# A hybrid SSD layer on one core: the gate and norm of the scans' output taken chunk by chunk inside the scan

## The chip, the cores and the metric

The kernel runs on one core of one Trainium2 chip. The metric is the device time of one execution in microseconds; the time before is the median of three runs. Engines are named as in the profile: PE (matmuls), PEld (weight loads into PE), DVE, ACT, POOL, and SP, whose queue issues most DMAs.

## The reference

One layer is run for 256 context tokens (the "prompt", p) and 1024 latent tokens (the "sample", s) with shared weights. All is float32. The part that the change touches is the second half of the mixer:

```python
xs, bm, cm = silu(conv(xbc))          # 512 channels of X, 2 groups x 128 of B and of C
dt_f, dt_b = softplus(dt + bias)      # 8 heads each, forward and backward
y = ssd_scan(x, dt_f, ...) + reversed(ssd_scan(reversed x, dt_b, ...)) + x * d_skip
y = rmsnorm(y * silu(z), g_ssd_norm)  # over the 512 channels
out = concat([out_a, y]) @ w_out      # out_a = gb * conv(gc * hc)
```

hc, gb, gc, z, xbc and dt are columns of one projection h @ w_in. The scans go in chunks of 128 tokens. A gated ConvFFN follows.

## The kernel before

Channels lie on the 128 partitions and tokens along the free dimension. Every large matmul is made of three float32r matmuls on split operands: hi is the rounded copy (an ACT Copy), lo the remainder (a subtraction on DVE or POOL), and a product is hi x hi + hi x lo + lo x hi (`mm3`, L153 to L164). A weight tile is loaded by SP into "raw" (`wload`, L144) and split by ACT (L149) and by POOL or DVE (L75 under `tt`). L75 and L78 are the helpers `tt` and `stt`, so nearly all DVE work has one of these two lines and is told apart by tile names.

One projection is 24 tiles of w_in; `proj_halves` (L360) issues it in two halves of four k each, so that other work can be put between. For the prompt all projections run in one stage (L697 to L713): eight of xbc, four of z (`zproj`), twelve for the four outputs `outa` of the short convolution. `dtstage` (L448) turns dt into decays: a chain of ACT (Exp, Ln) and DVE operations with its own table load at L211. `dttok` (L500) turns the result token-major on PE and builds a diagonal on DVE (L515) for one more matmul (L518).

For the sample, xbc is projected first. The eight halves of z and the 24 halves of `outa` form a generator, `fillers` (L747), a list of 32 pieces of PE work that are drawn one by one between the steps of the scan: one piece for each pair of chunks in pass 1 (the backward states, L773), then in pass 2 (`ssd_pass2`, L583) two pieces for the first two steps of the prompt and one for every other step. Pass 2 has two steps i per chunk, one per group. A step draws its piece, runs `output` (L639, matmuls at L652 into the PSUM tile "yp", then X = X * d_skip + yp on DVE), asks for csb two or three steps on, and prepares the masked decays wm and csb of the step after next (`prep`, L622). What is left of the pieces runs after the scan (L779).

z goes to DRAM: `zproj_halves` copies it out of PSUM on ACT (L405) and stores it with a DMA on ACT's queue (L406) as zd[j, :, tokens], four tiles j of 128 channels. After the scan `gate` (L790) runs for the prompt and then for the sample, at high priority, while the leftover pieces still run on PE: per j it loads z (L795), takes Silu (L796), multiplies into X, squares on ACT (L799, L802) and sums on DVE; a matmul with a tile of ones sums over partitions (`rstd`, L215, matmul at L221, Ln at L224, Exp at L226, table load at L211). Then X = X * g * r on DVE and the split into hi (ACT, L813) and lo (DVE, L814) into the tiles "ya" and "yb" that the out-projection reads.

The out-projection `wout` (L856) uses a new PSUM pool, opened at L826 after the old one is closed. Its x tiles and the conv outputs (tiles "oa", "ob") are loaded by SP at L832 to L842, behind the stores of the conv outputs at L438 and L439 in program order. The order on each engine is made by the framework's scheduler from the order of the program, priorities, and the edges that `after` (L205) adds. A queue or engine works in order.

Of the kernel before, what the change touches and what calls it, by code (L numbers as in the profile page):

```python
# [13 lines left out]
P = 128  # L14
# [4 lines left out]
L = 128  # L19
# [34 lines left out]
def body(nc, tc, A):  # L54
# [38 lines left out]
    def smv(n):  # L93
        a, b = SMO[n]
        return sm[:, a:b]
# [176 lines left out]

    def ada_block(k):
        wa = [T(xy, [P, 4, 2 * P], "xs", 4) for _ in range(2)]
# [76 lines left out]
    zd = T(dr, [4, P, TT], "zd", 1)  # L351
# [47 lines left out]
    def zproj_halves(s, j, lo_eng):  # L399
        g = proj_halves(s, 12 + j, lo_eng)  # L400
        next(g)
        yield
        pp = next(g)
        z = T(cv, [P, s.T], "xl", 2)
        act(z, pp, AF.Copy)  # L405
        nc.scalar.dma_start(zd[j, :, s.t0:s.t0 + s.T], z)  # L406
        yield
# [175 lines left out]
    def ssd_pass2(s, fill):  # L583
# [83 lines left out]
        for i in range(2 * s.nc):  # L667
            behind = fill(s, i)
            if i % 2 == 1 and i + 1 < 2 * s.nc:
                u.step(behind)  # L670
            output(*us[i], behind)
            load(i + 3)
            if i + 2 < 2 * s.nc:
                if i % 2 == 0:
                    u = front(i // 2 + 1)
                us.append((u, i % 2))
                prep(*us[-1])
        if s.name == "p":
            dma(A["o_stf"], sf[0])
# [12 lines left out]
    SS.X = [T(xy, [P, TS], "xs", 4) for _ in range(4)]  # L692
# [11 lines left out]
    silu = act(bcall, bcall, AF.Silu)  # L704
    for j in range(4):
        zproj(SP, j, PG if j % 2 else PV)
        if j == 0:
            dts = dtstage(SP, d4_p, silu)
    for j in range(4):
        for _ in outa(SP, j, PG):  # L710
            pass
        if j == 0:
            dttok(SP, *dts)  # L713
    dts = dtstage(SS, d4_s, silu)
# [40 lines left out]
    def fill(s, i):  # L755

        for _ in range(2 if s.name == "p" and i < 2 else 1):
            next(filler)
        return mid_mm[0]
# [13 lines left out]
    for i in range(0, len(scan), 2):  # L773
        cps = pairs(scan[i:i + 2])
        next(filler)
        steps(cps, (mid_mm[0], last_mm[-1]))
    ssd_pass2(SP, fill)
    ssd_pass2(SS, fill)
# [8 lines left out]
    g_gt, gt_ = open_pool("gt")  # L787
    mya = [[T(ya, [P, TA], "ya", 8, F32R) for _ in range(2)] for _ in range(4)]
    myb = [[T(yb, [P, OB], "yb", 8, F32R) for _ in range(2)] for _ in range(4)]
    def gate(s, behind):  # L790
        n = s.T
        acc = T(gt_, [P, n], "gq", 3)
        for j in range(4):
            z = T(gt_, [P, n], "gz", 2)
            dma(z, zd[j, :, s.t0:s.t0 + n])  # L795
            act(z, z, AF.Silu)  # L796
            tt(s.X[j], s.X[j], z, ALU.mult)
            if j == 0:
                act(acc, s.X[j], AF.Square)  # L799
            else:  # L800
                q = T(gt_, [P, n], "gq", 3)
                sq = act(q, s.X[j], AF.Square)  # L802
                tt(acc, acc, q, ALU.add)
        r = T(gt_, [P, n], "gq", 3)
        rstd(r, acc, n, pst, 512, sq, behind)
        for j in range(4):
            y = s.X[j]
            stt(y, y, smv("gsd")[:, j:j + 1], r, ALU.mult, ALU.mult)
            parts = [(0, n, mya, s.t0)] if s.name == "p" else \
                [(0, TA - TP, mya, TP), (TA - TP, TS, myb, 0)]  # L810
            for a, b, dst, o in parts:
                hi = dst[j][0][:, o:o + b - a]
                act(hi, y[:, a:b], AF.Copy)  # L813
                tt(dst[j][1][:, o:o + b - a], y[:, a:b], hi.bitcast(F32), ALU.subtract)  # L814
    with tc.high_priority():
        gate(SP, last_mm[-5])
        gate(SS, last_mm[-3])
    close_pool(g_xy)

    close_pool(g_gt)  # L820
# [394 lines left out]
```

## Time and profile before

| | us |
|---|---|
| median of 3 runs | 1587.39 |
| lowest, highest run | 1586.29, 1590.08 |
| profiled execution | 1587.93 |
| its span, first to last instruction | 1586.1 |
| PE busy / DVE busy / ACT busy / POOL busy | 1530.3 / 1101.8 / 648.0 / 514.7 |

The profile is of one execution; its times count from the span's start. A busy time is what an engine's own instructions cover; PE's is modelled from starts and sizes. PEclk is the clock granted to PE as a share of 2.4 GHz. The prompt's stage lies at about 76 to 160 us, pass 1 at about 237 to 290, pass 2 at 300 to 466, what remains of the pieces and the gate at 466 to 514, and the out-projection from 514.

### The profile page before, as it was taken

Reading aid. Unit: us, or ns where it says so; the run is one execution under the profiler, and the core shown is the slowest. Engines: PE = TensorE matmul, PEld = TensorE weight load, DVE = VectorE, ACT = ScalarE, POOL = GpSimd, SP = SyncE. Lnnn points to the kernel's source line nnn. Section 1 sums busy time; section 2 is a strip of 40 time slices with the busy share of each in tenths; the row PEclk is TensorE's granted clock in tenths of the full one; section 3 lists DMA queues with packets and bytes.
Section 4 is the critical chain, followed back from the end, with each engine's and each line's share of the span. In section 5 each row is a group of like instructions: output and inputs, shape, how many; then the busy total and the mean of one; then the engine's idle time right before and its main releaser. Section 6 shows DMA issues by size and latency. Waiting matters only on the chain. (4 is left out here: it accounts for less than half of the span.)

```text
span 1586.1 us, 24928 instructions
## 1 busy us (share of the span) xinstructions
PE 1530.3 (96%) x9942; PEld 1398.8 (88%) x9942; DVE 1101.8 (69%) x1637; ACT 648.0 (41%) x1005; POOL 514.7 (32%) x288
## 2 busy tenths in 40 slices
PE   6989999999997999999999999999999999999997
PEld 3688667888785899999999999999999999999996
DVE  5765626376867348797666796566798777987686
ACT  6553334355557134443333443333343232423333
POOL 0445001111110001444334434434455444444442
PEclk9999999999998999999999999999999999999998
DMA  8655554344334722322222252224432222432221
GB/s 301 214 183 169 208 199 158 115 140 133 120 103 148 286 67 82 111 76 83 76 80 66 96 176 80 73 74 143 139 98 82 93 81 94 143 96 86 70 62 67
DMA packets 81766, 193.19 MB, mean 122 GB/s; under 512 B 9298, under 2 KB 31474, under 8 KB 81650
## 3 DMA queue, kind: packets, MB, share of 16 engines
q1 hardware_dynamic: 79922, 188.46, 35.5%
q10 hardware_dynamic: 1728, 3.15, 0.5%
q8 instruction: 78, 1.28, 0.3%
q14 instruction: 38, 0.31, 0.1%
HBM read 167.89 MB, written 23.67 MB: 121 GB/s over the span
## 5 line engine op out<-in xcount | busy, mean ns | idle before, releaser
L78 DVE SCALAR_TENSOR_TENSOR cc<-acc,sm,cc 128x384 f32<-128x384 f32 (+7 forms) x836 | 547.1, 665 | 114.6 <-ACT cc L951 44.8
L75 POOL TENSOR_TENSOR wlo<-raw,whi 128x1024 fp32r<-128x1024 f32 (+2 forms) x83 | 192.6, 2321 | 682.6 <-ACT whi L149 544.4
L149 ACT ACTIVATE whi<-raw 128x1024 fp32r<-128x1024 f32 x90 | 95.2, 1058 | 233.0 <-PE acc L160 195.6
L78 DVE SCALAR_TENSOR_TENSOR x<-dn,mod,x 128x320 f32<-128x320 f32 (+2 forms) x176 | 96.1, 547 | 91.9 <-PE dn L162 91.1
L75 POOL TENSOR_TENSOR dlo<-draw,dhi 128x512 fp32r<-128x512 f32 (+1 forms) x88 | 107.6, 1224 | 78.3 <-ACT dhi L1008 78.3
L158 PE MATMUL acc<-ya,whi 128*128 128x256 f32 (+2 forms) x520 | 121.2, 315 | 11.9 <-ACT yb L813 8.4
L160 PE MATMUL acc<-ya,whi 128*128 128x256 f32 (+2 forms) x520 | 120.8, 314 | 0.0
L162 PE MATMUL acc<-ya,wlo 128*128 128x256 f32 (+2 forms) x520 | 120.3, 313 | 0.0
L158 PE MATMUL acc<-oa,whi 128*128 128x256 f32 (+2 forms) x520 | 119.3, 311 | 0.0
L160 PE MATMUL acc<-oa,whi 128*128 128x256 f32 (+2 forms) x520 | 119.3, 311 | 0.0
L162 PE MATMUL acc<-oa,wlo 128*128 128x256 f32 (+2 forms) x520 | 119.1, 311 | 0.0
L75 POOL TENSOR_TENSOR wlx<-raw,whx 128x1024 fp32r<-128x1024 f32 (+2 forms) x32 | 74.9, 2339 | 132.0 <-ACT whx L149 107.6
L158 PE MATMUL dn<-yb,dhi 128*128 128x320 f32 (+2 forms) x352 | 108.9, 310 | 1.8 <-DVE x L78 1.8
L162 PE MATMUL dn<-yb,dlo 128*128 128x320 f32 (+2 forms) x352 | 108.8, 309 | 0.0
L160 PE MATMUL dn<-yb,dhi 128*128 128x320 f32 (+2 forms) x352 | 108.7, 309 | 0.0
L158 PEld LDWEIGHTS acc<-ya,whi 128*128 128x128 f32 x520 | 93.8, 191 | 14.4 <-ACT yb L813 8.8
L158 PE MATMUL acc<-h,whi 128*128 128x512 f32 x320 | 104.7, 406 | 1.4 <-ACT whi L149 1.4
L162 PE MATMUL acc<-h,wlo 128*128 128x512 f32 x320 | 101.0, 396 | 1.6 <-POOL wlo L75 1.6
L160 PE MATMUL acc<-h,whi 128*128 128x512 f32 x320 | 101.4, 396 | 0.0
L1008 ACT ACTIVATE dhi<-draw 128x512 fp32r<-128x512 f32 (+1 forms) x88 | 52.9, 602 | 113.0 <-PE dn L160 53.6
L160 PEld LDWEIGHTS acc<-ya,whi 128*128 128x128 f32 x520 | 94.6, 192 | 2.2
L162 PEld LDWEIGHTS acc<-ya,wlo 128*128 128x128 f32 x520 | 94.2, 191 | 2.3 <-DVE wlo L75 0.2
(343 smaller groups left out, 3799.5 us busy)
## 6 DMA issues: line engine op xcount, KB each, us to landing
raw<-in_w_up SPq DMA_DIRECT2D x88, 512.0 KB, 3.5
x<-in_w_ada SPq DMA_DIRECT2D x32, 512.0 KB, 5.3
draw<-in_w_down SPq DMA_DIRECT2D x64, 256.0 KB, 2.7
x<-in_w_in SPq DMA_DIRECT2D x24, 512.0 KB, 3.6
raw<-in_w_in SPq DMA_DIRECT2D x22, 512.0 KB, 7.1
xs<-in_w_ad SPq DMA_DIRECT2D x16, 512.0 KB, 8.4
csb<-csds SPq DMA_DIRECT2D x16, 512.0 KB, 4.3
raw<-in_w_out SPq DMA_DIRECT2D x16, 512.0 KB, 3.6
```

The costliest lines, as they stand in the source:

```text
L75: (eng or V).tensor_tensor(out=out, in0=a, in1=b, op=op)
L78: V.scalar_tensor_tensor(out=out, in0=a, scalar=s, in1=b, op0=op0, op1=op1)
L149: act(hi, raw, AF.Copy)
L158: nc.tensor.matmul(o, wh[:, k, :], rh(k), start=k == 0, stop=False)
L160: nc.tensor.matmul(o, wh[:, k, :], rl(k), start=False, stop=False)
L162: mm = nc.tensor.matmul(o, wl[:, k, :], rh(k), start=False, stop=k == n - 1)
L1008: act(wh, raw, AF.Copy)
```

## The change

z is stored by chunk, zd[chunk, partition, j, token], with its Silu already taken at the eviction from PSUM. `gate` becomes a generator over a stretch of tokens with three steps: load z; multiply, square, add two of the four squared tiles to the other two; the matmul with ones over the remaining two, Ln, Exp, multiply by r. It has one instance for the prompt and one for each of the eight chunks of the sample. `post` draws its steps at the end of each step of pass 2: for chunk c the load two steps before the chunk's first, the second step after the chunk's last output, the third one step later; the last chunk's third step is drawn after the scan at high priority. The weight g moves into the split: hi is Copy with scale g, lo is X * g - hi in one DVE instruction.

The z tile of a gate takes a slot of the tag "cv" (four buffers), the tags of the gate's own pool are gone. X of the sample is one tile "xs" with four slices instead of four tiles. Pass 1 draws two pieces for each pair of chunks instead of one, pass 2 of the prompt two only at its first step; so all z of the sample is projected in pass 1, and three pieces remain after the scan instead of six. In the prompt's stage `dtstage` moves from behind the first z to inside the first `outa`, and `dttok` from behind the first `outa` to behind the second.

```diff
--- before.py
+++ after.py
@@ -270,8 +270,10 @@
     modv = mod.rearrange("p (b k) v -> p b k v", k=KT)
     badav = smv("bada").rearrange("p (b k) -> p b k", k=KT)
 
+    xq = T(xy, [P, 4, TS], "xs", 1)
+
     def ada_block(k):
-        wa = [T(xy, [P, 4, 2 * P], "xs", 4) for _ in range(2)]
+        wa = [xq[:, 2 * (k % 2) + i].rearrange("p (j c) -> p j c", j=4) for i in range(2)]
         for i in range(2):
             dma(wa[i], A["w_ad1"][k, i])
         pm = psa()
@@ -348,7 +350,7 @@
         sets.append(s)
     SP, SS = sets
     oad = T(dr, [4, 2, P, TT], "oad", 1)
-    zd = T(dr, [4, P, TT], "zd", 1)
+    zd = T(dr, [TT // L, P, 4, L], "zd", 1)
 
     last_mm, mid_mm = [], [None]
 
@@ -402,8 +404,9 @@
         yield
         pp = next(g)
         z = T(cv, [P, s.T], "xl", 2)
-        act(z, pp, AF.Copy)
-        nc.scalar.dma_start(zd[j, :, s.t0:s.t0 + s.T], z)
+        s.zact = act(z, pp, AF.Silu)
+        nc.scalar.dma_start(zd[s.t0 // L:s.t0 // L + s.nc, :, j].rearrange("c p l -> p c l"),
+                            z.rearrange("p (c l) -> p c l", l=L))
         yield
 
     def outa(s, j, lo_eng):
@@ -580,7 +583,7 @@
             dma(st[0], A["st"][:, 1])
         return [(copies, step, c) for c in range(s.nc - 1, -1, -1)]
 
-    def ssd_pass2(s, fill):
+    def ssd_pass2(s, fill, post):
 
 
         sf = [None]
@@ -675,6 +678,7 @@
                     u = front(i // 2 + 1)
                 us.append((u, i % 2))
                 prep(*us[-1])
+            post(i)
         if s.name == "p":
             dma(A["o_stf"], sf[0])
 
@@ -689,7 +693,7 @@
     SP.B, SP.C = bcp[0:2], bcp[2:4]
     SS.hi = lambda k: hs_hi[k]
     SS.lo = lambda k: hs_lo[k]
-    SS.X = [T(xy, [P, TS], "xs", 4) for _ in range(4)]
+    SS.X = [xq[:, i] for i in range(4)]
     d4_s = dtcopy(SS, pd_s)
     for i in range(N_LOOP):
         xbc(SS, i, SS.X[i], PG)
@@ -701,17 +705,16 @@
             dtmm(pd_p, range(KT), lambda k: xp[k // 4][:, k % 4], TP)
             d4_p = dtcopy(SP, pd_p)
     act(xall, xall, AF.Silu)
-    silu = act(bcall, bcall, AF.Silu)
+    act(bcall, bcall, AF.Silu)
     for j in range(4):
         zproj(SP, j, PG if j % 2 else PV)
-        if j == 0:
-            dts = dtstage(SP, d4_p, silu)
     for j in range(4):
-        for _ in outa(SP, j, PG):
-            pass
-        if j == 0:
+        for i, _ in enumerate(outa(SP, j, PG)):
+            if i == j == 0:
+                dts = dtstage(SP, d4_p, SP.zact)
+        if j == 1:
             dttok(SP, *dts)
-    dts = dtstage(SS, d4_s, silu)
+    dts = dtstage(SS, d4_s, SP.zact)
 
 
     bcs = [T(sd, [P, TS], "bc", 4) for _ in range(4)]
@@ -754,7 +757,7 @@
 
     def fill(s, i):
 
-        for _ in range(2 if s.name == "p" and i < 2 else 1):
+        for _ in range(2 if s.name == "p" and i == 0 else 1):
             next(filler)
         return mid_mm[0]
 
@@ -773,9 +776,58 @@
     for i in range(0, len(scan), 2):
         cps = pairs(scan[i:i + 2])
         next(filler)
-        steps(cps, (mid_mm[0], last_mm[-1]))
-    ssd_pass2(SP, fill)
-    ssd_pass2(SS, fill)
+        mid_mm[0] = last_mm[-1]
+        next(filler)
+        steps(cps, (last_mm[-2], last_mm[-1]))
+
+    def gate(x, c0, n):
+
+        z = T(cv, [P, 4, n], "cv", 4)
+        for c in range(n // L):
+            dma(z[:, :, c * L:(c + 1) * L], zd[c0 + c])
+        yield
+        tt(x, x, z, ALU.mult)
+        act(z, x, AF.Square)
+        tt(z[:, 0:2], z[:, 0:2], z[:, 2:4], ALU.add)
+        yield
+        pp = psa()
+        for i in range(2):
+            mm = nc.tensor.matmul(pp[:, 0:n], ones, z[:, i], start=i == 0, stop=i == 1)
+            if i == 0:
+                after(mm, last_mm[-1])
+        r = z[:, 2]
+        act(r, pp[:, 0:n], AF.Ln, scale=1.0 / 512, bias=epsc)
+        act(r, r, AF.Exp, scale=-0.5)
+        tt(x, x, r.unsqueeze(1).broadcast_to([P, 4, n]), ALU.mult)
+        yield
+
+    gate_p = gate(xall, 0, TP)
+    gates = [gate(xq[:, :, c * L:(c + 1) * L], SP.nc + c, L) for c in range(SS.nc)]
+
+    def post_p(i):
+        if i == 2 * SP.nc - 1:
+            next(gate_p)
+
+    def post_s(i):
+
+        c = i // 2
+        if i == 0:
+            next(gate_p)
+            next(gates[0])
+        if i == 1:
+            next(gate_p)
+        if i % 2 == 1:
+            next(gates[c])
+        else:
+            if c > 0:
+                next(gates[c - 1])
+            if c + 1 < SS.nc:
+                next(gates[c + 1])
+
+    ssd_pass2(SP, fill, post_p)
+    ssd_pass2(SS, fill, post_s)
+    with tc.high_priority():
+        next(gates[-1])
     for _ in filler:
         pass
     close_pool(g_sw)
@@ -784,40 +836,17 @@
 
     g_ya, ya = open_pool("ya")
     g_yb, yb = open_pool("yb")
-    g_gt, gt_ = open_pool("gt")
     mya = [[T(ya, [P, TA], "ya", 8, F32R) for _ in range(2)] for _ in range(4)]
     myb = [[T(yb, [P, OB], "yb", 8, F32R) for _ in range(2)] for _ in range(4)]
-    def gate(s, behind):
-        n = s.T
-        acc = T(gt_, [P, n], "gq", 3)
-        for j in range(4):
-            z = T(gt_, [P, n], "gz", 2)
-            dma(z, zd[j, :, s.t0:s.t0 + n])
-            act(z, z, AF.Silu)
-            tt(s.X[j], s.X[j], z, ALU.mult)
-            if j == 0:
-                act(acc, s.X[j], AF.Square)
-            else:
-                q = T(gt_, [P, n], "gq", 3)
-                sq = act(q, s.X[j], AF.Square)
-                tt(acc, acc, q, ALU.add)
-        r = T(gt_, [P, n], "gq", 3)
-        rstd(r, acc, n, pst, 512, sq, behind)
-        for j in range(4):
-            y = s.X[j]
-            stt(y, y, smv("gsd")[:, j:j + 1], r, ALU.mult, ALU.mult)
-            parts = [(0, n, mya, s.t0)] if s.name == "p" else \
-                [(0, TA - TP, mya, TP), (TA - TP, TS, myb, 0)]
-            for a, b, dst, o in parts:
-                hi = dst[j][0][:, o:o + b - a]
-                act(hi, y[:, a:b], AF.Copy)
-                tt(dst[j][1][:, o:o + b - a], y[:, a:b], hi.bitcast(F32), ALU.subtract)
     with tc.high_priority():
-        gate(SP, last_mm[-5])
-        gate(SS, last_mm[-3])
+        for x, dst, o in ((xall, mya, 0), (xq[:, :, 0:TA - TP], mya, TP), (xq[:, :, TA - TP:], myb, 0)):
+            n = x.shape[2]
+            for j in range(4):
+                g = smv("gsd")[:, j:j + 1]
+                hi, lo = [t[:, o:o + n] for t in dst[j]]
+                act(hi, x[:, j], AF.Copy, scale=g)
+                stt(lo, x[:, j], g, hi.bitcast(F32), ALU.mult, ALU.subtract)
     close_pool(g_xy)
-
-    close_pool(g_gt)
     close_pool(g_cv)
     close_pool(g_hs)
     close_pool(g_ps)
```

## Rows read from the trace of the kernel before

**Rows 1.** The page's first part: busy time, share of the span and number of instructions of an engine.

```profile
PE 1530.3 (96%) x9942; PEld 1398.8 (88%) x9942; DVE 1101.8 (69%) x1637; ACT 648.0 (41%) x1005; POOL 514.7 (32%) x288
```

**Rows 2.** The list of waits of PE over the whole span: what waited, for whom, us in total, times, the longest.

```profile
PE yp L241 <- DVE cv L75: 11.4, 1, 11.4
PE acc L158 <- ACT yb L813: 8.4, 1, 8.4
PE acc L158 <- ACT whi L149: 4.9, 2, 3.5
PE acc L158 <- ACT xl L405: 3.3, 1, 3.3
PE sa L518 <- DVE cv L515: 3.3, 1, 3.3
...
PE acc L162 <- POOL wlo L75: 1.6, 1, 1.6
...
PE sa L530 <- DVE xd L75: 1.3, 1, 1.3
...
PE sa L533 <- ACT sb L554: 1.1, 1, 1.1
```

**Rows 3.** The timeline of PE from the last pieces to the out-projection: start, length, line, operation, how many were merged, and in brackets the idle time before it and what ended it.

```profile
489.75 0.73 PE L158 MATMUL acc<-h,whi 128*128 128x512 f32 x2 [1.38 <-ACT whi L149]
...
492.57 1.22 PE L162 MATMUL acc<-h,wlo 128*128 128x512 f32 x2 [1.63 <-POOL wlo L75]
...
505.55 0.62 PE L162 MATMUL acc<-h,wlo 128*128 128x512 f32 x2
514.57 0.93 PE L158 MATMUL acc<-ya,whi 128*128 128x256 f32 x2 [8.40 <-ACT yb L813]
...
543.58 0.96 PE L158 MATMUL acc<-ya,whi 128*128 128x256 f32 x2 [3.54 <-ACT whi L149]
```

**Rows 4.** Windows: the stretch, its length, busy us (and instructions) of each engine, the clock granted to PE as a share of full, the share of the DMA engines, GB/s.

```profile
120.00:124.00 4.00, 4.00 (x23) 4.00 (x23) 0.42 (x1) 2.75 (x5) 2.70 (x2) 0.58 0.39 131
...
340.00:460.00 120.00, 119.05 (x779) 97.19 (x777) 92.10 (x118) 68.46 (x154) 17.15 (x7) 1.00 0.34 115
...
488.00:492.00 4.00, 1.57 (x6) 0.67 (x4) 4.00 (x4) 4.00 (x6) 2.22 (x1) 1.00 0.40 131
492.00:496.00 4.00, 3.42 (x9) 2.78 (x10) 4.00 (x4) 2.10 (x3) 0.52 (x1) 0.57 0.39 131
...
512.00:516.00 4.00, 1.43 (x5) 1.37 (x6) 4.00 (x6) 2.19 (x3) 0.00 (x0) 0.50 0.00 1
516.00:520.00 4.00, 4.00 (x17) 3.75 (x16) 3.04 (x3) 0.00 (x0) 0.00 (x0) 0.58 0.92 325
...
544.00:548.00 4.00, 4.00 (x18) 3.63 (x18) 2.02 (x2) 0.78 (x1) 0.00 (x0) 0.67 0.47 147
```

**Rows 5.** The timeline of DVE in the prompt's stage, in pass 2 and after the scan: start, length, line, operation, shape.

```profile
109.20 4.53 DVE L75 TENSOR_TENSOR cv<-cv,cv 40x256 f32<-40x256 f32 x2 [1.23 <-ACT cv L467]
...
428.12 0.68 DVE L75 TENSOR_TENSOR wm<-sa,wm 128x512 f32<-128x512 f32 x1
...
458.04 0.68 DVE L75 TENSOR_TENSOR wm<-sa,wm 128x512 f32<-128x512 f32 x1
...
496.13 1.27 DVE L78 SCALAR_TENSOR_TENSOR cv<-cv,sm,cv 128x1023 f32<-128x1023 f32 x1
...
508.40 0.62 DVE L75 TENSOR_TENSOR ya<-xs,ya 128x448 fp32r<-128x448 f32 x1
508.94 0.75 DVE L75 TENSOR_TENSOR yb<-xs,yb 128x576 fp32r<-128x576 f32 x1
...
513.21 1.22 DVE L75 TENSOR_TENSOR cv<-acc,cv 128x1024 f32<-128x1024 f32 x1
```

**Rows 6.** The timeline of ACT, the same columns.

```profile
117.68 0.42 ACT L488 ACTIVATE cv<-cv 40x256 f32<-40x256 f32 x1 [4.39 <-DVE cv L487]
...
335.68 2.45 ACT L630 ACTIVATE wm<-wm,toks 128x128 f32<-128x128 f32 x8 [2.48 <-DVE wm L75]
...
478.38 1.28 ACT L796 ACT_TABLE_LOAD   x1
479.68 1.06 ACT L796 ACTIVATE gz<-gz 128x1024 f32<-128x1024 f32 x1
...
513.81 0.67 ACT L813 ACTIVATE yb<-xs 128x576 fp32r<-128x576 f32 x1
```

**Rows 7.** The timeline of PE in pass 2 and behind it: outputs (L652) of steps, the first matmuls of a half of a projection, and the ones-matmul of the prompt's gate.

```profile
433.13 0.43 PE L652 MATMUL yp<-wm,xd 128*64 128x128 f32 x2
...
458.23 0.73 PE L158 MATMUL acc<-h,whi 128*128 128x512 f32 x2
...
463.94 0.43 PE L652 MATMUL yp<-wm,xd 128*64 128x128 f32 x2
...
476.78 0.59 PE L221 MATMUL yp<-gq,ones 128*128 128x256 f32 x2
```

**Rows 8.** The timeline of SP's DMA queue: start of the issue, its length, line, transfer, how many.

```profile
515.54 0.32 SPq L438 DMA_DIRECT2D oad<-xl  x1
...
520.24 5.62 SPq L838 DMA_DIRECT2D x<-in_xT  x8
...
531.80 84.12 SPq L147 DMA_DIRECT2D raw<-in_w_out  x13
```

## The prediction

> **What bounds the kernel now.** I read the engine table first. PE is busy 1530.3 of 1586.1 us and DVE, the next of the computing engines, 69% [rows 1], so time can be won where PE stands or runs at half clock, and lost where new work on another engine makes PE late. 0.3% of this kernel is 4.8 us, about what a measurement can tell from no change: that is the bound for the chances below.
>
> Next the list of PE's waits. Besides the kernel's first wait (11.4 us, not touched), the long ones are 8.4 us, a group of two with 4.9 us whose longest is 3.5, two of 3.3 and one of 1.6 [rows 2]. The timeline of PE puts four of them around the end of the scan: 1.38 and 1.63 us inside the last six halves of projections, 8.40 us before the first matmul of the out-projection, 3.54 us before its fourth weight tile [rows 3]. They sum to 14.95 us. The windows show what else they cost: the granted clock is 0.57, 0.50, 0.58 and 0.67 in the stretches behind them, that is, much of each runs at the 1.2 GHz level. Time busy times missing clock is 3.42 x 0.43 + 1.43 x 0.50 + 4 x 0.42 + 4 x 0.33 = 5.2 us: 1.5 behind the first two waits, 2.4 behind the third, 1.3 behind the fourth [rows 4].
>
> Why the 8.40 us? PE is done with the last projection at about 506.2 (last pair 505.55 + 0.62). DVE then works off the gate's last part, multiplies and splits, and only at 513.21 the eviction of that projection's PSUM, which ends at 514.43. ACT's last split ends at 514.48, and PE starts at 514.57 [rows 3, 5, 6]. The new PSUM pool follows the old one, so of the two ends I read the eviction as the one that PE needs; either way it is the gate of 1024 tokens, serial after the scan, that PE waits for.
>
> **The change, part by part.**
>
> *The gate moves into the scan.* Removed from the end: the Silu, products, squares and sums of 1280 tokens, with the table switches between Silu, Ln and Exp, 1.28 us each [rows 6]. What stays there is the last chunk's norm and the split. So the ACT and POOL waits of 1.38 and 1.63 us, which come while ACT and DVE run gate work ahead of a weight tile's hi and lo, should go: -3.0, and -1.5 of clock.
>
> *What the end of the scan then holds.* Three halves instead of six lie behind the last output (26 of 32 pieces were consumed before it, 29 are now). One half is 5.7 us (458.23 to 463.94) [rows 7], so there are 17.1 us of cover. DVE has in it: the last gate (two products of 0.68 and a shorter sum, 1.8), the split (priced as the splits of before: 4 x 0.62 and 4 x 0.75 for the sample, 4 x 0.4 for the prompt by its columns, 7.1), one product and two taps of the convolution (1.22 + 2 x 1.27 = 3.8), a weight's lo (1.2) and one collision with POOL (1.8: two small products took 4.53 us at 109.20) [rows 5]. Sum 15.7. It fits, barely; the split of the prompt and of the first 448 tokens can run before the last output. Then the eviction follows PE's last matmul: 1.22 plus handovers, a wait of 1.5 us for 8.40. Saved 6.9, and the 2.4 of clock, since behind the lone wait of 1.38 us no clock was missing until the second came (1.00 in 488 to 492) [rows 3, 4]. If the cover fails, this eviction is late next; the far end is 3.5 us more.
>
> *The fourth out-projection tile.* Its weights are issued at 531.80, behind the store of the last conv output (515.54) and eight loads of x [rows 8]. If everything stays behind that store, PE comes 2.4 us earlier relative to it (no half clock) and the wait grows from 3.5 to about 5.9. If the x loads go ahead, because the buffers they reuse (X among them) come free with the split, before PE ends, it vanishes and takes its 1.3 of clock along. Bounds +2.4 and -4.8; I take -2.0, nearer to the second, since the gate's own pool, which overlaid these addresses, is gone.
>
> *Sums of squares on PE.* Before, the ones-matmuls stream 1280 columns; after, 2560, as each chunk's squares are summed to two tiles and PE adds those. 256 columns take 0.59 us with their start [rows 7], some 0.45 of PE's pace: +2.2.
>
> *Scan.* Per chunk DVE gets 1.8 us, ACT a square (0.6 by the 0.67 of 576 columns), a Ln and an Exp (0.3 each, an eighth of 2.45) and perhaps table loads [rows 6]. Over 340 to 460 us DVE is busy 92.1 and ACT 68.5 of 120 [rows 4]. Two chunks take 30.8 us (433.13 to 463.94, four outputs apart) [rows 7], so one is 15.4; DVE goes from 11.8 to 13.6 in it and ACT from 8.8 to 10.0, or 12.6 with two loads of 1.28. Neither fills the chunk. What must not be late is wm: its last write ends at 428.80 for the output at 433.13, and at 458.72 for the one at 463.94, so 4.3 and 5.2 us ahead [rows 5, 7]. The gate's steps are written behind the next prep, and their burst of 3.8 on ACT, loads included, stays within that. Bounds 0 and +6 (a few outputs late by 1 to 2 us); I take +1.0. Two couplings lie in this bound: a gate's z takes a slot of the four "cv" buffers that the convolution's u and v share, and ten z loads (eight before) stand in SP's queue, where one that waits for its slot holds up the weight and csb loads behind it.
>
> Whether the Ln in a gate reloads is not visible: every Ln in the gate of before has a load written out at L211, and the new gate has none. Bounds 0 and 2 x 1.28 per gate; I take the upper. In the trace a load takes 1.28 and the next ACTIVATE starts 0.02 us later (478.38 to 479.68) [rows 6].
> The Trainium skill ("ScalarE: Activation LUTs", What ACT_TABLE_LOAD costs) gives about 2.66 us per switch, a drain of some 1.38 included; the rows show no such drain. By the page ACT would reach 15.3 us per chunk.
>
> *Pass 1.* Two halves now lie between the chunk pairs, not one, and the two state steps stand half a projection apart. The waits of 1.3 and 1.1 us [rows 2] are for a PSUM buffer of the neighbouring step or copy. Bounds 0 and -2.4; I take -1.5, more than half, as the steps' distance is what such a wait lacks. The z evictions get Silu for Copy, 1.06 us at 1024 columns [rows 6], right behind the last Silu of B and C.
>
> *Prompt stage.* dtstage moves behind all z of the prompt and dttok behind the second conv output. Today ACT stands 4.39 us on dtstage's last Ln, with z's eviction behind it, because DVE is slow (the 4.53 us above, beside POOL), and PE waits 3.3; then 3.3 for dttok's diagonal, with a clock of 0.58 between [rows 2, 4 to 6]. After the move the same chain runs beside the conv outputs, whose evictions take z's place behind that Ln, with POOL making every lo. I see no reason for either sign: 0, with -8 if both waits and the 1.7 of clock go, +8 if they double.
>
> *At nothing:* the smaller pieces of the z stores (eight, issued on ACT's queue as before, loaded long after), the slices of one "xs" tile for four, g as a scale in the split (same instructions, one multiply less).
>
> **Sum.** -3.0 - 1.5 - 6.9 - 2.4 - 2.0 + 2.2 + 1.0 - 1.5 + 0 = -14.1 us. The profiled execution took 1587.9 (span 1586.1, 1.8 around it), 0.5 above the median of 1587.4; 1587.9 - 14.1 = 1573.8, against the median 1573.3: 1573.5.
>
> **Rivals.**
> *Transfers give it back.* The order at the end stays, so the fourth tile waits 5.9 us: -14.1 + 2.0 + 2.4 = -9.7, 1578. For: today's order on SP. Against: x need not stay behind the stores.
> *The prompt stage decides.* Its 8 us either way: 1565.5 or 1581.5. For: that is where ACT's order is rewritten. Against: nothing in the rows favours a side.
> *Slower: ACT in the scan.* ACT works in order. If a gate's Ln, waiting for its ones-matmul behind half a projection, stands ahead of a prep's Exps, and both reloads follow, prep is late by up to 5.7 + 3.8 = 9.5 us against 4.3 to 5.2 of slack; PE late by some 3 us a chunk on average is 24 over eight. It decides once the delay passes the slack. -14.1 + 23 = +9: 1597. For: such blocking in order is what holds ACT 4.39 us at 113 [rows 6]. Against: the matmul is issued a whole step before its Ln is needed.
> By the page's 2.66 us the slack would be passed sooner.
> *The change does not do what it says*: the last chunk's chain and the split fill the end as the whole gate did, the 8.40 us stay, pass 1 gives little: 1584 to 1588. For: DVE's 15.7 of 17.1. Against: half of the split can be done before the last output.
>
> **How the numbers follow.** Forecast 0.52, transfers 0.18, prompt stage better 0.06, worse 0.07, slower 0.12, nothing 0.05. Faster (below 1582.6): 0.52 + 0.18 + 0.06 and a little of the others, 0.77; slower (above 1592.2): 0.12; between: 0.11. The range, 1562 to 1588, takes in the better prompt stage with a little more, the failed transfers, the worse prompt stage and the change that does nothing, and leaves out the slow rival.
>
> **What would show it.** Right: a wait of some 1.5 us before the first out-projection matmul with the granted clock at 1.00 behind it; no Silu table between Ln and Exp at the end; three halves after the last output; pass 1's waits gone or shorter; PE full through the scan. Wrong: PE waits for wm or csb in the scan; pairs of table loads with ACT idle ahead of prep's Exps; a wait over 4 us on whi in the out-projection; new waits between 100 and 140 us.

## The result, and the profile after

The median went from 1589.27 us (1585.79 to 1592.32) to 1592.48 (1588.68 to 1595.39), 21 runs of each: a ratio of 1.0019 [1.0012, 1.0027]. The change made the kernel some 3 us slower, where 14 us faster were forecast. The profiled span went from 1586.1 to 1588.3 us.

The page's first part of the changed kernel, against [rows 1]:

```profile
PE 1531.2 (96%) x9972; PEld 1399.9 (88%) x9972; DVE 1096.9 (69%) x1642; ACT 660.2 (42%) x1023; POOL 514.9 (32%) x288
```

Nearly nothing moved in the sums; ACT has 12 us more. What moved is where PE stands. The list of PE's waits of the changed kernel:

```profile
PE acc L158 <- ACT cv L421: 7.0, 1, 7.0
PE acc L158 <- ACT whi L149: 4.7, 1, 4.7
PE sa L795 <- DVE cv L75: 3.6, 4, 1.3
PE sa L521 <- DVE cv L518: 3.6, 1, 3.6
PE sa L533 <- DVE xd L75: 2.5, 2, 1.3
...
PE acc L158 <- DVE cv L75: 1.4, 1, 1.4
```

The 8.4 us on yb and the waits of 1.4 and 1.6 us in the last halves [rows 2, 3] are gone; 1.4 us are left before the out-projection. But 7.0 us stand where z's eviction cost 3.3 before, the fourth tile still waits, and a new line, L795, waits: the ones-matmul of the gates. The timeline of PE puts them in place (columns as in [rows 3]):

```profile
124.36 0.58 PE L158 MATMUL acc<-bc,whi 128*128 128x256 f32 x1 [7.03 <-ACT cv L421]
...
488.09 0.71 PE L795 MATMUL sa<-cv,ones 128*128 128x128 f32 x4 [1.32 <-DVE cv L75]
498.73 0.71 PE L795 MATMUL sa<-cv,ones 128*128 128x128 f32 x4 [1.10 <-DVE cv L75]
514.60 0.56 PE L158 MATMUL acc<-ya,whi 128*128 128x256 f32 x2 [1.41 <-DVE cv L75]
...
543.52 0.96 PE L158 MATMUL acc<-ya,whi 128*128 128x256 f32 x2 [4.65 <-ACT whi L149]
```

Windows of the changed kernel (columns as in [rows 4]): the clock behind the end of the scan is whole now, behind the fourth tile's wait it is at half.

```profile
512.00:516.00 4.00, 2.59 (x15) 2.00 (x14) 2.77 (x3) 2.96 (x3) 0.00 (x0) 1.00 0.16 64
516.00:520.00 4.00, 4.00 (x27) 3.83 (x26) 1.85 (x2) 0.00 (x0) 0.00 (x0) 1.00 0.84 290
544.00:548.00 4.00, 4.00 (x15) 3.57 (x15) 1.95 (x2) 0.70 (x1) 0.00 (x0) 0.50 0.47 163
```

To see where the time lies, both spans are cut at matmuls that both kernels have: the first of the prompt's stage, the first of the sample's xbc, the first transpose of pass 1 (of the prompt's X, at 237.3 and 240.7 us), the first of the out-projection, the first of the FFN behind it.

| stage, us | before | after | difference |
|---|---|---|---|
| ahead of the prompt's stage | 71.3 | 69.9 | -1.4 |
| prompt's stage | 88.0 | 93.0 | +5.0 |
| sample's xbc | 78.0 | 77.8 | -0.2 |
| pass 1, pass 2, rest of the pieces | 277.3 | 273.9 | -3.4 |
| out-projection | 197.8 | 198.4 | +0.5 |
| behind it (the change doesn't touch it) | 873.7 | 875.3 | +1.6 |

The last row and the first vary by such amounts between other kernels below, too. So two things ask for a reason: the prompt's stage lost 5.0 where 0 was taken, and the stretch from pass 1 to the out-projection won 3.4 where the terms made 12.1 (3.0 + 1.5 + 6.9 + 2.4 + 1.5, less 2.2 and 1.0). The fourth tile's 2.0 did not come either.

### The profile page after: what moved, and what is told of

The parts are those of the page before. It is cut to its first block, busy times and chain, and to the rows that moved or that the text cites. A ratio compares the mean times of both kernels' runs of the same rounds, so it can differ in the third digit from the quotient of the medians.

```text
span 1588.3 us, 25016 instructions
## 1 busy us (share of the span) xinstructions
PE 1531.2 (96%) x9972; PEld 1399.9 (88%) x9972; DVE 1096.9 (69%) x1642; ACT 660.2 (42%) x1023; POOL 514.9 (32%) x288
## 3 DMA queue, kind: packets, MB, share of 16 engines
q8 instruction: 78, 1.28, 0.3%
## 5 line engine op out<-in xcount | busy, mean ns | idle before, releaser
L78 DVE SCALAR_TENSOR_TENSOR cc<-acc,sm,cc 128x384 f32<-128x384 f32 (+7 forms) x836 | 547.2, 665 | 115.5 <-ACT cc L980 45.7
```

What stands on the lines that cost most here:

```text
L78: V.scalar_tensor_tensor(out=out, in0=a, scalar=s, in1=b, op0=op0, op1=op1)
```

## The experiments

Each was timed beside the kernel before, and its ratio is to that; two kernels' ratios are subtracted and taken by 1590 us for a difference between them, which is uncertain by 2 to 3 us (by 4 between the two kernels of the last experiment). Times of stages come from one profile each.

### The move of dtstage and dttok alone, in the kernel before

```diff
     for j in range(4):
         zproj(SP, j, PG if j % 2 else PV)
-        if j == 0:
-            dts = dtstage(SP, d4_p, silu)
     for j in range(4):
-        for _ in outa(SP, j, PG):
-            pass
-        if j == 0:
+        for i, _ in enumerate(outa(SP, j, PG)):
+            if i == j == 0:
+                dts = dtstage(SP, d4_p, silu)
+        if j == 1:
             dttok(SP, *dts)
```

> The kernel before with one part of the change: dtstage of the prompt moves into the first conv output, dttok behind the second; z, gate and the order of the pieces stay. Theory (slots): dtstage holds all four cv buffers, so the first conv output's copy out of PSUM waits for one of them; PE stands some 7 us before the third projection of the first conv output in place of 3.3 before the fourth z, the wait for dttok's diagonal stays near 3.5, and the kernel is 3 to 6 us slower than before. Rival (the stage is neutral, the loss sits elsewhere): within 1 us of before, two waits of 3 to 4 us.

Measured: 1593.81 us, ratio 1.0021 [1.0008, 1.0034]; prompt's stage 93.0 us. The list of PE's waits of this kernel:

```profile
PE acc L158 <- ACT yb L812: 8.4, 1, 8.4
PE acc L158 <- ACT cv L418: 7.0, 1, 7.0
...
PE sa L518 <- DVE cv L515: 3.6, 1, 3.6
```

The 8.4 us of the end are still there, and both waits of the changed kernel's prompt stage have come. So the 5.0 us belong to this move and to nothing else of the change.

### dtstage and dttok behind all of the prompt's work

The changed kernel, with the prompt's dtstage behind its last outa and its dttok, then the sample's dtstage, behind the next xbc tile; the sample's dttok comes one tile later.

```diff
-        for i, _ in enumerate(outa(SP, j, PG)):
-            if i == j == 0:
-                dts = dtstage(SP, d4_p, SP.zact)
-        if j == 1:
-            dttok(SP, *dts)
-    dts = dtstage(SS, d4_s, SP.zact)
+        for _ in outa(SP, j, PG):
+            pass
+    dts = dtstage(SP, d4_p, SP.zact)
...
         xbc(SS, i, xbcs[i], PV)
+        if i == N_LOOP:
+            dttok(SP, *dts)
+            dts = dtstage(SS, d4_s, SP.zact)
...
```

> The kernel after, with dtstage of the prompt behind all twelve projections of the conv outputs, in the stage where the sample's xbc is projected and POOL is idle; its dttok and the sample's dtstage follow the first xbc tile there, the sample's dttok comes one tile later. Theory: the waits of 7.0 and 3.6 us and their half clock (about 2 us) go and nothing takes their place: 9 to 13 us faster than after, 6 to 10 faster than before. Rival (dtstage costs PE the same wherever it stands, as the chain is on DVE): waits of 5 us or more in the new place, within 3 us of after.

Measured: 1579.67 us, ratio 0.9934 [0.9920, 0.9948], 13.5 us below the changed kernel. Both waits are gone, and the windows over the prompt's stage say it in one line each, the changed kernel first, then this one:

```profile
69.90:162.90 93.00, 80.82 (x616) 75.88 (x613) 47.40 (x67) 46.07 (x67) 46.24 (x20) 0.94 0.54 173
```

```profile
70.30:146.28 75.98, 74.39 (x605) 71.64 (x602) 37.45 (x48) 42.12 (x58) 46.51 (x20) 1.00 0.65 210
```

PE stands 1.6 us instead of 12.2, and its busy time falls by 6.4, at a clock of 1.00 against 0.94 and with 11 matmuls less, which lie in the next stage. The next stage takes up the dt work for 4.8 us (82.6 against 77.8).

### A buffer of its own for the copy that PE waits for

In the changed kernel the row that ends the 7.0 us is ACT's copy of the first outa's first projection out of PSUM. These are rows of its ACT, DVE and POOL timelines around it:

```profile
117.30 1.06 ACT L149 ACTIVATE whi<-x 128x1024 fp32r<-128x1024 f32 x1 [0.53 <-PE acc L160]
123.21 0.42 ACT L491 ACTIVATE cv<-cv 40x256 f32<-40x256 f32 x1 [4.86 <-DVE cv L490]
123.92 0.38 ACT L421 ACTIVATE cv<-acc 128x256 f32<-128x256 f32 x1 [0.29 <-DVE cv L483]
```

```profile
116.80 4.43 DVE L75 TENSOR_TENSOR cv<-cv,cv 40x256 f32<-40x256 f32 x2 [0.97 <-ACT cv L470]
```

```profile
116.09 2.38 POOL L75 TENSOR_TENSOR wlx<-x,whx 128x1024 fp32r<-128x1024 f32 x1 [1.78 <-ACT whx L149]
118.43 2.52 POOL L75 TENSOR_TENSOR wlo<-x,whi 128x1024 fp32r<-128x1024 f32 x1
```

The copy waits last for L483, dtstage's second scan: dtstage holds all four "cv" buffers, and the copy needs one. So I took this slot for the cause, and gave the copy a buffer of its own.

```diff
-        u = T(cv, [P, n], "cv", 4)
+        u = T(cv, [P, n], "up", 1) if s.name == "p" and j == 0 else T(cv, [P, n], "cv", 4)
```

> The changed kernel with one tile more: the prompt's first u (the copy at L421) has a buffer of its own and no longer takes one of the four that dtstage holds; dtstage and dttok stay where the change put them. Theory (the slot alone holds the copy, and with it the PSUM tile that PE needs): the 7.0 us wait goes, the 3.6 us wait of dttok's diagonal stays between 1 and 4 us, the prompt stage shrinks from 93.0 to 84 to 87 us, and the kernel is 5 to 9 us below the changed one (0.9955 to 0.998 of the kernel before the change). Rival (ScalarE's order holds it: the chain of dtstage stands ahead of whatever has to be evicted): a wait of 4 us or more stays in this place, prompt stage 90 us or more, within 3 us of the changed kernel.

Measured: 1590.09 us, ratio 1.0002 [0.9989, 1.0015]; prompt's stage 92.7 us. The theory that this slot alone holds PE fell. Rows of PE, ACT and DVE of this kernel:

```profile
129.40 0.55 PE L158 MATMUL acc<-bc,whi 128*128 128x256 f32 x1 [6.12 <-DVE cv L75]
```

```profile
115.15 0.36 ACT L421 ACTIVATE up<-acc 128x256 f32<-128x256 f32 x1
...
123.76 0.42 ACT L491 ACTIVATE cv<-cv 40x256 f32<-40x256 f32 x1 [5.21 <-DVE cv L490]
124.08 1.04 ACT L149 ACTIVATE whi<-x 128x1024 fp32r<-128x1024 f32 x1
125.03 0.49 ACT L429 ACTIVATE cv<-up,sm 128x256 f32<-128x256 f32 x1
```

```profile
123.75 0.68 DVE L483 TENSOR_TENSOR_SCAN cv<-cv,cv 8x256 f32<-8x256 f32 x1
...
125.30 2.52 DVE L75 TENSOR_TENSOR cv<-cv,cep 40x256 f32<-40x256 f32 x1
127.74 0.99 DVE L78 SCALAR_TENSOR_TENSOR cv<-up,sm,cv 128x255 f32<-128x255 f32 x2
128.83 0.42 DVE L75 TENSOR_TENSOR cv<-acc,cv 128x256 f32<-128x256 f32 x1
```

The copy is done at 115.5, nearly nine us earlier, and PE gets a few tiles further, to stand for 6.12 us at a later eviction of the same outa: its second product on DVE (128.83), behind the taps (127.74), which come behind dtstage's last product (125.30) and need ACT's L429, which stood behind dtstage's Ln. An outa takes three ACT and five DVE operations; a z takes one ACT operation. Beside outa, dtstage's chain stands in the order of both engines.

This does not clear the slots, though. What L429 writes, the v of the same outa, is a "cv" tile as well. Of the four it can only have the buffer that u had in the changed kernel, and dtstage's second scan L483 gives that back at 124.43 us, 0.6 us before L429 starts. A z needs none of these buffers (its tile is "xl"), an outa needs two, and this run freed one. What the slots cost and what the order costs is not told apart.

### How much of it is DVE beside POOL

In [rows 5] and above, two products of 40x256 took 4.43 to 4.53 us while POOL made a lo. Here the lo of the prompt's first two outa is made on DVE, in the changed kernel.

```diff
-        for i, _ in enumerate(outa(SP, j, PG)):
+        for i, _ in enumerate(outa(SP, j, PG if j > 1 else PV)):
```

> The changed kernel with the lo parts of the weights of the prompt's first two outa made on DVE instead of POOL; dtstage and dttok stay inside them. In the changed kernel two products of 40x256 that dtstage does on DVE took 4.43 us beside two POOL subtractions of 2.4 us, where 0.42 each is what such a product takes with POOL idle. Theory (POOL's subtraction stretches DVE's small products, and that makes dtstage's chain long enough to hold PE): the pair takes 0.9 to 1.3 us, the 7.0 us wait falls to 2 to 4 us although DVE has six subtractions of 1.2 us more, the prompt stage shrinks from 93.0 to 87 to 90 us, and the kernel is 3 to 6 us below the changed one. Rival (the chain holds PE by its place in the order of DVE and ACT, however long its products are): prompt stage 92 us or more, the kernel within 2 us of the changed one or slower.

Measured: 1587.69 us, ratio 0.9987 [0.9976, 0.9997]; prompt's stage 91.8 us. DVE's and PE's rows:

```profile
117.56 0.86 DVE L75 TENSOR_TENSOR cv<-cv,cv 40x256 f32<-40x256 f32 x2
```

```profile
122.57 0.58 PE L158 MATMUL acc<-bc,whi 128*128 128x256 f32 x1 [4.87 <-ACT cv L421]
```

The pair took 0.86 us, as the theory wanted, and the wait fell by 2.2 us, less than it wanted; the stage came out at the rival's bound. So the stretching by POOL is a part, some 2 of the 7 us net of the subtractions that DVE got in exchange; that the place of the chain is the rest is not shown apart from the "cv" slots. (Its ratio is 5 us below the changed kernel's, the span 2.7; the stage accounts for 1.2.)
The Trainium skill ("GPSIMD Engine Reference", Specifications) says that GpSimd's (POOL's) interfaces to SBUF are shared with VectorE (DVE) and that VectorE's instructions with two SBUF inputs contend for them; the pair of products, at 4.43 against 0.86 us, agrees.

### The x loads behind the weight tiles

SP's queue in the changed kernel, from the store of the last conv output (columns as in [rows 8]):

```profile
515.79 0.32 SPq L441 DMA_DIRECT2D oad<-xl  x1
...
522.73 4.15 SPq L867 DMA_DIRECT2D x<-in_xT  x8
...
532.49 19.83 SPq L147 DMA_DIRECT2D raw<-in_w_out  x5
```

It is the order of before: the eight loads of x stand between the stores and the fourth weight tile, with loads of oa and ob among them. Here five of them, and the loads of ob, are issued between the weight tiles.

```diff
-    for k in range(KT):
+    for k in range(3):
         dma(x1[k], xT[:, k, :])
-    for j in range(4):
-        for i in range(2):
-            dma(mob[j][i].bitcast(F32), oad[j, i, :, TA:TT])
...
+            if t0 == 0 and m >= 3:
+                dma(x1[m], xT[:, m, :])
+                if m >= 4:
+                    for i in range(2):
+                        dma(mob[m - 4][i].bitcast(F32), oad[m - 4, i, :, TA:TT])
```

> The kernel after, with the order of loads behind the scan changed: x tiles 3 to 7 and the conv outputs of the second block are issued behind the weight tile with which they are used, not ahead of all of them. Theory (order on SP's queue): the fourth weight tile is there in time, its wait of 4.65 us and 3 us of half clock go: 5 to 8 us faster than after, 2 to 5 faster than before. Rival (bandwidth): the same bytes have to come in, the wait moves to x or to a later tile, within 2 us of after.

Measured: 1582.74 us, ratio 0.9958 [0.9945, 0.9972], 9.7 us below the changed kernel, more than the theory's 5 to 8. The 4.65 us are gone, and SP's queue shows why: behind the store there are weights at 516.50, 519.41 and 530.07 instead of a first one at 532.49.

```profile
516.50 0.38 SPq L147 DMA_DIRECT2D raw<-in_w_out  x1
...
519.41 0.78 SPq L147 DMA_DIRECT2D raw<-in_w_out  x1
...
530.07 0.33 SPq L147 DMA_DIRECT2D raw<-in_w_out  x1
```

The stage of the out-projection takes 190.7 us against 198.4: 7.7 us for a wait of 4.65, since the stretch behind it runs at the whole clock too (540 to 560 us at 1.00, in the changed kernel at 0.83).

### One table for Ln and Exp

ACT in one chunk of the changed kernel: eight Exps of wm and one of csb, the gate's square, and then Ln and Exp with a table load ahead of each.

```profile
391.72 2.45 ACT L633 ACTIVATE wm<-wm,toks 128x128 f32<-128x128 f32 x8 [3.46 <-DVE wm L75]
394.07 1.04 ACT L635 ACTIVATE csb<-csb 128x1024 f32<-128x1024 f32 x1
395.02 0.62 ACT L790 ACTIVATE cv<-xs 128x512 f32<-128x512 f32 x1
...
399.49 1.28 ACT L799 ACT_TABLE_LOAD   x1
400.79 0.37 ACT L799 ACTIVATE cv<-sa,epsc 128x128 f32<-128x128 f32 x1
401.05 0.59 ACT L545 ACTIVATE xd<-sa 128x512 f32<-128x512 f32 x1
401.66 1.28 ACT L800 ACT_TABLE_LOAD   x1
402.96 0.31 ACT L800 ACTIVATE cv<-cv 128x128 f32<-128x128 f32 x1
```

Each of the nine gates has two loads, 18 in all, which is the upper bound that the prediction took. Here one load of the table with both functions is written out ahead of the loop over the prompt's chunks in pass 2 (the function at L211 that `rstd` calls), and the Exps of `prep` are ordered behind it. Over the whole kernel there are 28 table loads before the change, 40 after it and 22 here.

```diff
...
-            act(csb, csb, AF.Exp)
...
+            e = act(csb, csb, AF.Exp)
+            if sw_tab[0] is not None:
+                after(e, sw_tab[0])
...
+        if s.name == "p":
+            sw_tab[0] = lnexp_table(SS.zact)
```

> The kernel after, with one table load written out ahead of pass 2 that serves both Ln and Exp, so that the 18 loads in the gates go (23 us of ACT). Theory (reloads make the gate late): PE's waits for the gate's sums (4.3 us in all) shrink to under 1.5 us and the last gate is 2.6 us earlier: 2 to 4 us faster than after. Rival (the order on ACT and DVE makes it late, the square stands behind eight Exps): the waits stay above 3 us, within 1 us of after.

Measured: 1584.59 us, ratio 0.9967 [0.9955, 0.9979], 8.3 us below the changed kernel: the mechanism as expected, twice its size. ACT now has 0.35 and 0.32 us there (400.74, 401.46) and no load, and no wait at the ones-matmul is left. Windows over the sample's chunks of pass 2, the changed kernel and then this one:

```profile
349.50:494.40 144.90, 140.62 (x925) 114.02 (x924) 118.28 (x161) 108.73 (x221) 20.83 (x8) 1.00 0.38 130
```

```profile
352.90:491.80 138.90, 138.84 (x925) 114.31 (x924) 115.97 (x161) 88.11 (x202) 19.01 (x8) 1.00 0.40 130
```

The same 925 matmuls: PE stood 4.3 us and stands 0.1, and its busy time falls by another 1.8 us at a clock of 1.00 in both. So each short wait costs more than its own length: set against the same matmuls here, a wait of 0.62 us put what follows back by 0.77 us, the one of 1.32 us by 1.48 us.
The Trainium skill ("ScalarE: Activation LUTs", Table sets: the hidden batching unit) counts one load for Ln then Exp, since one set holds both; the trace of the changed kernel shows two, and one only where the load of that set was written out.

### The gate's third step one step later

The changed kernel, with Ln, Exp and scaling, and the next load of z, drawn one step of pass 2 later; the loads of the tables stay.

```diff
         if i % 2 == 1:
-            next(gates[c])
-        else:
             if c > 0:
                 next(gates[c - 1])
+            next(gates[c])
             if c + 1 < SS.nc:
                 next(gates[c + 1])
```

> The changed kernel with the gate's third step (the Ln, the Exp and the scaling by the rstd) one scan step later, and the load of the next z with it; nothing else. Theory (the table loads themselves are what the scan's waits come from, wherever in the chunk they fall on ScalarE's queue): the 18 loads stay, ScalarE's burst of square, two loads and two ACTIVATEs is only split, the waits of the x matmuls (L795 in the changed kernel) shrink from 1.3 to 0.5 us or less each, and of the 8.4 us that one written-out load brought, 2 to 5 come back: 0.997 to 0.9985 of the changed kernel. Rival (only the place in the queue counts): all of the waits go and the gain is that of the one load, 7 to 9 us. Second rival (the place counts for nothing): within 1.5 us of the changed kernel, the waits at the later step.

Measured: 1591.71 us, ratio 1.0008 [0.9996, 1.0020], not to be told from the changed kernel. One wait at L795 is left on PE, at the last gate:

```profile
498.21 0.71 PE L795 MATMUL sa<-cv,ones 128*128 128x128 f32 x4 [3.15 <-DVE cv L75]
```

So the place in the queue does count: from the first transpose of the sample's X to the last output it takes 237.3 us (changed kernel 239.4, one table 233.4). But it isn't all. In the scan PE now waits for xd, wm and X instead, 3.1 us in all where the changed kernel has 0.8 for such. And the last chunk's gate does not come earlier with the scan's end: on DVE the last update of X (495.72) stands behind eight splits into ya (from 489.92), and the last ones-matmul starts at 498.21, in the changed kernel at 498.73. From the last output to the out-projection it takes 22.7 us against 20.2. Moving the step gains 2.2 of the 6.0 us that the loads cost in the scan, and gives them back at the end. None of the three forecasts had that.

### The new distribution of the pieces, with the old gate

The kernel before, with two pieces for each pair in pass 1 and the gate behind the scan as one block. With three pieces left instead of six, the ones-matmuls of the gate are put behind the last two of them.

```diff
-        for _ in range(2 if s.name == "p" and i < 2 else 1):
+        for _ in range(2 if s.name == "p" and i == 0 else 1):
...
         next(filler)
-        steps(cps, (mid_mm[0], last_mm[-1]))
+        mid_mm[0] = last_mm[-1]
+        next(filler)
+        steps(cps, (last_mm[-2], last_mm[-1]))
...
-        gate(SP, last_mm[-5])
-        gate(SS, last_mm[-3])
+        gate(SP, last_mm[-2])
+        gate(SS, last_mm[-1])
```

> The kernel before with one part of the change alone: its new distribution of the split's pieces (two for each pair of steps in the first pass, the rest at the end), while gate and norm stay behind the scan as one block. Theory (the gate is a serial chain, the 8.4 us wait was what the pieces of work around it left open): with fewer products to run beside the gate the wait ahead of the out projection grows to 17 to 25 us, and the kernel is 8 to 16 us slower than before. Rival (the pieces were spread for ScalarE's and VectorE's sake and TensorE has as much beside the gate as it had): within 3 us of before.

Measured: 1590.59 us, ratio 1.0005 [0.9992, 1.0017]. The number is the rival's, but PE does stand longer:

```profile
511.38 2.07 PE L221 MATMUL yp<-gq,ones 128*128 128x512 f32 x2 [12.96 <-DVE gq L75]
514.23 2.08 PE L221 MATMUL yp<-gq,ones 128*128 128x512 f32 x2 [0.78 <-ACT gq L224]
517.08 0.80 PE L158 MATMUL acc<-ya,whi 128*128 128x256 f32 x2 [0.78 <-ACT gq L224]
520.10 0.74 PE L158 MATMUL acc<-ya,whi 128*128 128x448 f32 x1 [2.01 <-ACT ya L815]
```

That is 16.5 us of waits against 8.40 + 1.38 + 1.63 [rows 3], and 267.4 us from the first transpose of the sample's X to the out-projection against 262.9. The out-projection gives 2.8 us back (195.0 against 197.8): two more weight tiles go out ahead of the loads of x (509.77 and 513.21), and the fourth tile's wait is gone. The gate is serial, but my forecast of 17 to 25 us was too long, and I had not counted what follows. The new place of the ones-matmuls does not make the 12.96 us: PE was through with its last piece at 498.42, and the gate's sum came at 511.38.

### The three edits together with the new gate, and two of them with the old

The changed kernel with the edits of the late dt stage, the late x loads and the one table together:

> The changed kernel with the three side effects taken away together: the prompt's dt stage behind its xbc work, the x loads of the last stretch behind their weight tiles, and one written-out load of the table that holds both Ln and Exp ahead of the second pass. Theory (the three lie in different stages and add): 13.5 + 9.8 + 8.4 = 31.7 us below the changed kernel, about 1561 us, 0.980 to 0.984 of the kernel before. Rival (two of them ended the same wait, or the clock takes some back): 1567 to 1573 us.

And the kernel before with the late dt stage and the late x loads, the gate as it was:

> The kernel before with the two edits that have nothing to do with the gate: the dt stage of the prompt behind its xbc work, and the x loads of the last stretch behind their weight tiles. The gate and norm stay as they were. It gives the price of the chunk-by-chunk gate alone when it is set beside the run with all three side effects taken away. Theory (the gate chunk by chunk is worth what the stretch from the scan to the out projection showed, 10.7 us): this kernel at about 1571 us, 0.987 to 0.992 of before, and the other 9 to 12 us below it. Rival (the gain of the gate is given back behind the out projection once the loads are in order): the two within 3 us of each other.

Measured: 1564.05 us, ratio 0.9834 [0.9813, 0.9854], with the new gate; 1577.20 us, ratio 0.9915 [0.9896, 0.9933], with the old one. The three edits take 29.4 us off the changed kernel, nearly their sum (31.5 by the ratios above). They are not all side effects of the change: the late dt stage and the late x loads take 13.5 us off the kernel before, too, which had waits of 3.3 and 3.3 us in the prompt's stage and of 3.54 at the fourth tile already [rows 2, 3]. The windows of the first of the two, over its chunks of pass 2 and from there to the out-projection, show a full PE:

```profile
339.50:478.50 139.00, 138.91 (x925) 114.25 (x924) 116.00 (x161) 88.32 (x202) 19.03 (x8) 1.00 0.39 131
478.50:497.31 18.81, 17.40 (x80) 13.92 (x77) 11.54 (x16) 7.87 (x11) 0.00 (x0) 1.00 0.58 190
```

Between the kernels with the new and with the old gate lie 0.0081 of the ratio, 13 us, of which the stretch from pass 1 to the out-projection makes 9.9 (266.6 against 276.5). That is what taking gate and norm chunk by chunk is worth in this kernel, with the new distribution of the pieces and the one table load.

## Why the prediction was wrong

**What held.** The gate behind the scan was what PE waited for. The 8.40 us became 1.41, the waits of 1.38 and 1.63 us in the last halves and the half clock behind both went, as the steps had it (-6.9, -2.4, -3.0, -1.5). With the table loads taken out, the stretch from pass 1 to the out-projection is 266.6 us (one table alone) against 277.3, 10.7 less, where the terms made 12.1, or 13.1 without the scan's +1.0.

**The prompt's stage**, "the same chain runs beside the conv outputs, whose evictions take z's place behind that Ln": 0 was taken, +5.0 came; the move alone costs 0.21% [0.08%, 0.34%]. The step failed in taking one eviction for another. A z leaves PSUM by one ACT operation, an outa takes three on ACT and five on DVE, and two of the "cv" buffers of which dtstage holds all four. So dtstage's chain now stands ahead of PE's evictions in two queues, and in the buffers. PE's wait of 3.3 us became one of 7.0; the 3.3 for dttok's diagonal stayed, at 3.6. The bounds of 8 us either way held the 5.0, and moving the chain away altogether, with the waits of before, was worth 13.5. Which of the three holds PE most is open: giving one buffer back moved the wait, taking away POOL's part shortened it by 2.2 us.

**The scan**, +1.0 within 0 and +6: taking the loads out gave back 7.4 us by the profiles (6.0 in the scan, the far end of the bounds, and 1.4 behind it), 8.3 by the ratios. The loads were counted rightly (two per gate, 1.28 us each, the upper of two bounds between which no row decided) and the slack of wm held: no output waits for wm in the list of PE's waits. What the step left out is that the change puts a matmul of its own into PE's order, the ones-matmul, and this has a deadline too. Its input is the sum of squares, whose square stands on ACT behind nine Exps (395.02 above), and what the loads add to ACT's queue arrives there. The question of what must not be late was asked of wm alone. It is not the whole of the 7.4: with the step moved, the waits at the ones-matmul in the scan went, and PE waited for xd, wm and X instead, so ACT's loads make other inputs late as well. The slower rival saw ACT's queue as the place, but let wm be late, at 24 us.

**The fourth out-projection tile**, -2.0 between +2.4 and -4.8: its wait grew by 1.1 us, at a half clock in 544 to 548. The x loads did not go out early; they are behind the stores and ahead of the weights in SP's order, as before. That was the rival "transfers give it back", which had the place right: with the order changed, 9.7 us came.

**Pass 1**, -1.5: the wait for "xd" came twice instead of once (2.5 us against 1.3), and with the old gate and the new distribution of the pieces too, and the 1.1 us for "sb" stayed at 1.0. The wait for "xd" lies between the copies of a pair's two chunks, which still stand back to back; the second half comes behind them and gives them no distance.

In sum: -14.1 forecast, +2.2 in the span. The prompt's stage makes 5.0 of the 16.3 between them, the table loads 6.4 more than the term for the scan, the fourth tile 2.5, pass 1 and the rest of it the remainder, with the stages that the change doesn't touch. Two of the signs that the prediction named for being wrong came: the wait over 4 us on whi in the out-projection (4.65) and a new wait between 100 and 140 us (7.0).

## What to carry to other kernels

When work is moved into a stretch that is full, ask for the deadline of every instruction that it puts into the bounding engine's own queue, not only of those that were there. When a chain is moved beside other work, compare the two neighbours by the engines and buffers that they use: the chain is the same, the neighbour is not. And where two functions of ACT alternate, look for the load of the table that holds both, written out; here 18 loads of 1.28 us were the price of its absence.

## What the runs showed of the hardware

- Two products of 40x256 on DVE took 4.43 us beside POOL's subtraction of 128x1024, and 0.86 us with POOL idle.
- Short waits of PE (up to 1.3 us) cost more than themselves even at the whole clock: with the table loads gone, 4.2 us of idle time went in 145 us, and 1.8 us of PE's busy time (which is modelled) with it, for the same 925 matmuls.
- A stage with a wait of 4.65 us on PE got 7.7 us shorter when it went; behind the wait the granted clock was 0.50, that is the 1.2 GHz level.
